# Gate rows spread by DMA instead of TensorE, GLA levels on half the columns, and loads other than weights issued by GpSimd, in an mLSTM + GLA decoder step

## The chip, the cores and the metric

One NeuronCore of one Trainium2 chip runs the whole step. The metric is device time in microseconds of one execution; the numbers given are medians over runs on the chip. All arithmetic is in float32, of which the large matrix products are made from pairs of "fp32r" parts (a rounded high part and the rest).

## The reference, cut to what matters

One layer on 256 prompt tokens and 8 decode sequences of one token each (264 columns in all), model width 2048:

- `p = x @ w_in` with some 13,000 output columns. They feed an mLSTM branch (q, k, v, input and forget gates, output gates), a GLA branch (q, k, v, a low-rank gate, an output gate) and two merge gates.
- mLSTM, 4 heads of 256: `b = cumsum(logf)`, `m_t = max(b + m, max_s(b_t - b_s + itil_s))`, weights `w = exp(b_t - b_s + itil_s - m_t)`, `num = (q k^T * w) v`, `h = num / max(|den|, exp(-m_t))`. With u = b - m (one value per head and prompt token) and r = itil - b, the weight is `exp(u_t + r_s)`: u has to stand in every partition, as a row over t, and so has exp(-m).
- GLA, 4 heads of 128: `a = sum_d q_t k_s exp(bc_t - bc_s)` for s <= t, built here in levels: at level l, blocks of 2^l tokens, each even block s meets the odd block t beside it.
- The decode states (mLSTM C, 8.4 MB; GLA S, 4.2 MB) are read, updated with the new token and written back.
- Norms, gates, two branch projections, the merge, one output projection and a LayerNorm over `ALPHA * x + y`.

## The kernel before, in words

The tokens are columns: x stands in SBUF as 16 tiles of 128 channels by 264 tokens. Output columns of the weights are taken in units of 128; `units()` lists 129 of them (16 qk, 1 small with the gates, 8 av, 4 bq, 4 bk, 8 bv, 16 ao/az, 8 bz, 32 ga/gb, 16 pab, 16 out). A unit is 16 k-tiles of three matmuls each (`parts`, lines 223, 224 and 227: high times high, high times low of x, low times high), that is 48 matmuls of 264 columns.

The weights come as pieces of half a unit (512 KB) through SyncE's queue (`load_raw`, line 181), into four buffers; `cast_piece` makes the high part on ScalarE (line 203) and the rest on VectorE (line 204), into five buffers each, three pieces ahead of the unit that TensorE works on (`LA`).

TensorE's order is the order of the program (`manual_schedule`). The other engines are ordered by a scheduler with priorities, each engine's stream being fixed when the kernel is built. Between two units `pump` moves the side work on: it steps generators, each up to its next `yield`, as far as a budget of 2.8 goes. The generators that matter here:

- `g_gates` (from line 279): gates of the mLSTM. It makes m, b, u, r in 16 partitions (lines 316 to 336), transposes r, and then makes `dmx` = exp(-m) in all 128 partitions by eight matmuls with a selecting matrix `selr` (lines 377 and 378, in two steps with a `yield` after each).
- `g_a_prompt`: mLSTM on the prompt. For each head, `s1` makes the scores (line 420) and beside them spreads u over the partitions by four matmuls with `selr` (line 423); line 427 adds r and the causal limit.
- `g_a_decode`: the decode states, 16 chunks of 512 KB: `load` (line 526), rows of k and q spread from DRAM (`spread_rows`, line 489), decay on ScalarE (line 555), update and product on VectorE (lines 571 and 573), store through GpSimd's queue (line 564).
- `g_gla_prompt`: seven levels; each has its products on TensorE (line 707), scalings of Q and K on VectorE (line 714) and a copy under a mask into `am` (line 730).
- `g_gla_decode`: 8 chunks (`load`, line 778) with rows of three kinds (`rows_of`, line 489), VectorE lines 807 to 810, store through GpSimd (line 813).

All large tiles beside the weights share a pool of 20 slots (`b4`); a load into a slot waits until whatever stood there has been used or stored. All loads go through SyncE's queue, in order, so weights and the loads of the side work stand in one line; GpSimd's queue carries most stores and a few small operations.

Of the kernel before, what the change touches and what calls it, by code (L numbers as in the profile page):

```python
# [13 lines left out]
F32 = mybir.dt.float32  # L14
# [7 lines left out]
L = 256  # L22
# [3 lines left out]
H = 4  # L26
# [57 lines left out]
def body(ctx, tc, xT, wbig, wsmall, par, cmask, lmask, sel, rowc, gate, wgu, cT, sT, nst, cst, lnr,  # L84
# [152 lines left out]
    st, sel_t = {}, {}  # L237
# [41 lines left out]

    def g_gates(ps):  # L280
# [36 lines left out]
        gr = lambda n: tmp.tile([16, T], F32R, tag="t1", name=n, bufs=T1_BUFS)  # L317
        mh_, ml_, uh, ul = gr("mhi"), gr("mlo"), gr("uhi"), gr("ulo")
        selr = t4([16, 8, 128], "selr", F32R)
        A.copy(out=selr, in_=sel_t["sel"])  # L320
# [13 lines left out]
        split(mh_, ml_, m)  # L334
        split(uh[:, 0:L], ul[:, 0:L], u[:, 0:L])
        st.update(uh=uh, ul=ul, selr=selr)
# [4 lines left out]
        for w, src in ((0, r), (1, wk)):  # L341
            for s in range(2):
                o = w * 32 + s * 16
                PE.transpose(out=pt[:, o:o + 16], in_=src[:, s * 128:(s + 1) * 128], identity=ident[0:16, 0:16])
        dm = one.tile([16, H, NB], F32, tag="dm", name="dm")
# [26 lines left out]
        em = t4([128, H, T], "dmx")  # L372
        st["dmx"] = em
        for hh in (0, 2):
            for h in (hh, hh + 1):
                pp = side_ps()[:, 0:T]
                PE.matmul(pp, lhsT=selr[:, h, :], rhs=mh_, start=True, stop=False)
                PE.matmul(pp, lhsT=selr[:, h, :], rhs=ml_, start=False, stop=True)
                A.activation(out=em[:, h, :], in_=pp, func=AF.Exp, scale=-1.0)
            yield 1.0  # L380
# [27 lines left out]
    def g_a_prompt():  # L408
        qT, kT, vt = st["qT"], st["kT"], st["avt"]
        uh, ul, selr, rw, dmx = st["uh"], st["ul"], st["selr"], st["rw"], st["dmx"]  # L410
# [75 lines left out]
    def spread_rows(dst, src):  # L486

        n = src.shape[0] * src.shape[1]
        nc.sync.dma_start(out=dst.rearrange("p b d -> p (b d)"),  # L489
                          in_=src.rearrange("r d -> (r d)").unsqueeze(0).to_broadcast([128, n]))  # L490

    def g_a_decode():
# [14 lines left out]
        nc.sync.dma_start(out=nr, in_=nst)  # L507
# [3 lines left out]
        for x, src in enumerate((kr, qr)):  # L511
            nc.sync.dma_start(out=kq_d[x], in_=src)
# [149 lines left out]
    def g_gla_rows():  # L662
        gq, gk, la = st["gq"], st["gk"], st["la"]
        gd = one.tile([128, 3, H, NB], F32, tag="gd", name="gd")
        A.activation(out=gd[:, 0], in_=la[:, :, L:T], func=AF.Exp, scale=TAU_INV)
        V.tensor_copy(out=gd[:, 1], in_=gk[:, :, L:T])
        V.tensor_copy(out=gd[:, 2], in_=gq[:, :, L:T])
        yield 0.4
        pt = side_ps()
        PE.transpose(out=pt[0:96, 0:128], in_=gd.rearrange("p x h b -> p (x h b)"), identity=ident)  # L670
        rows = tmp.tile([96, 128], F32, tag="t1", name="rows", bufs=T1_BUFS)
        A.copy(out=rows, in_=pt[0:96, 0:128])
        rows_d = dram.tile([96, 128], F32, name="rows_d")
        nc.sync.dma_start(out=rows_d, in_=rows)
        st["rows"] = rows_d
        yield 0.3

    def g_gla_prompt():
# [19 lines left out]
        for l in range(7):  # L698
            hs = 1 << l
            pl = side3(8, 64)  # L700
            for hf in range(2):
                for h in range(H):
                    for s0, n0, w in {32: ((0, 0, 32), (64, 32, 32)), 64: ((0, 0, 64),)}.get(hs, ((0, 0, 64), (64, 0, 64))):
                        m = min(hs, 64) if hs >= 32 else 64
                        rhs = Q[:, h, hf * 128:hf * 128 + 128].rearrange("p (n two s) -> p n two s", two=2, s=hs)[
                            :, n0 // hs:(n0 + w) // hs, 1, :]
                        PE.matmul(pl[s0:s0 + m, 4 * hf + h, n0:n0 + w].rearrange("p (n s) -> p n s", s=hs),  # L707
                                  lhsT=K[:, h, hf * 128 + s0:hf * 128 + s0 + m], rhs=rhs, start=True, stop=True)
# [11 lines left out]
            av = am.rearrange("p a (n two s) -> p a n two s", two=2, s=hs)[:, :, :, 1, :]  # L720
# [5 lines left out]
            if hs == 64:  # L726
# [3 lines left out]
            V.copy_predicated(out=av, mask=lm_sb[:, l, :].rearrange("p (n s) -> p n s", s=hs).unsqueeze(1).to_broadcast(  # L730
                [128, 8, 64 // hs, hs]), data=pl.rearrange("p a (n s) -> p a n s", s=hs))
# [39 lines left out]
    def g_gla_decode():  # L771
# [168 lines left out]
    def g_ln_rows():  # L940
# [3 lines left out]
        for hf in range(2):  # L944
            gf, hi = t4([128, 1024], "lgf"), t4([128, 1024], "lgh", F32R)
            gg = t4([128, 1024], "lgg", F32R)
            nc.sync.dma_start(out=gf, in_=lnr[:, hf * 1024:hf * 1024 + 1024])
# [4 lines left out]
            nc.sync.dma_start(out=bb, in_=lnr[64:65, hf * 1024:hf * 1024 + 1024].to_broadcast([128, 1024]))  # L952
# [150 lines left out]
    with tc.manual_schedule(engines=MANUAL):  # L1103
# [20 lines left out]
        for n, (kind, j) in enumerate(UN):  # L1124
# [15 lines left out]
            else:  # L1140
# [3 lines left out]
                if n == 4:  # L1144
                    V.tensor_copy(out=im_sb, in_=ident)
                    sel_t["sel"] = t4([16, 8, 128], "sel_sb")
                    for dst, src in ((gate_sb, gate), (wgu_sb, wgu), (sel_t["sel"], sel), (rc_sb, rowc), (cm_sb, cmask), (lm_sb, lmask)):
                        nc.sync.dma_start(out=dst, in_=src)
# [41 lines left out]
def _layout(v):  # L1190
# [51 lines left out]
    sel = np.zeros((16, 8, 128), np.float32)  # L1242
    for st in range(2):
        for h in range(4):
            for p in range(128):
                sel[(2 * st + p // 64) * 4 + h, st * 4 + h, p] = 1.0
    d["sel"] = sel
# [63 lines left out]
```

## Time and profile before

| | us |
|---|---|
| median of three runs | 845.92 (845.65 to 849.77) |
| the profiled execution | 848.47 |
| its span, first to last instruction | 846.7 |
| TensorE busy in it | 826.7 (98%) |
| VectorE busy | 591.4 (70%) |
| ScalarE busy | 451.4 (53%) |
| GpSimd busy | 45.1 (5%) |
| share of the span in which the 16 DMA engines moved data of SyncE's queue | 61.3% |
| the same for GpSimd's queue | 4.3% |

The profiled execution lies 1.77 us outside its span (848.47 - 846.7), and 2.55 us above the median. A matmul's record is longer than the distance to the next one, since they are pipelined: it is the starts that tell what one costs.

### The profile page before, as it was taken

How to read it: one execution, taken by the hardware profiler on the slowest of the kernel's cores; microseconds unless marked ns; L12 is line 12 of the kernel's file. 1: busy time of each engine (PE TensorE's matmuls, PEld its weight loads, DVE VectorE, ACT ScalarE, POOL GpSimd, SP SyncE). 2: the span in 40 equal slices, each digit the busy share in tenths (PEclk: the TensorE clock that was granted, in tenths of full speed). 3: DMA queues.
4: the chain of work that ended last, by engine and by line, in shares of the span. 5: the costliest groups of instructions: out<-in, count | busy, mean ns of one | idle time of the engine just before them, and what ended most of it. 6: DMA issues, size and time to landing. Idle time of an engine off the chain costs nothing.

```text
span 846.7 us, 16717 instructions
## 1 busy us (share of the span) xinstructions
PE 826.7 (98%) x6773; PEld 813.3 (96%) x6773; DVE 591.4 (70%) x964; ACT 451.4 (53%) x706; POOL 45.1 (5%) x75
## 2 busy tenths in 40 slices
PE   6999999999999999999999998999999999999996
PEld 6999999999899999999999998999999999999995
DVE  6877668545658788757579979994445766666962
ACT  5655457545445653555467747764444444444633
POOL 0000000000001000001000000310000000000410
PEclk9999999999999999999999998999999999999998
DMA  8765565558586985678687799756555555576513
GB/s 318 246 203 181 159 188 171 165 163 262 214 284 225 381 292 189 198 262 312 203 300 243 231 335 329 240 171 203 184 178 184 185 177 177 185 248 214 176 49 103
DMA packets 54766, 184.76 MB, mean 218 GB/s; under 512 B 8209, under 2 KB 9153, under 8 KB 54689
## 3 DMA queue, kind: packets, MB, share of 16 engines
q1 hardware_dynamic: 50560, 169.28, 61.3%
q0 software_dynamic: 4128, 14.42, 4.3%
q8 instruction: 53, 0.87, 0.4%
q14 instruction: 25, 0.20, 0.1%
HBM read 166.98 MB, written 16.69 MB: 217 GB/s over the span
## 4 chain that ended last, share of the span: by engine, by line
PE 81%; DMA 7%; DVE 6%; ACT 2%; issue 2%; SPq 1%; ACTq 0%; POOLq 0%; POOL 0%; DVEq 0%
PE mm L223 25%; PE mm L224 25%; PE mm L227 24%; DMA raw<-wbig 4%; DMA cch<-cT 4%; DVE lo L204 2%; ACT hi L203 1%; DVE scr L573 1%; PE sd L707 1%; PE sd L464 1%; DVE cch L571 1%; ACT cch L555 1%; PE sd L754 0%; SPq L489 0%; PE sd L420 0%
## 5 line engine op out<-in xcount | busy, mean ns | idle before, releaser
L223 PE MATMUL mm<-xh,hi 128*128 128x264 f32 x1552 | 447.2, 289 | 10.2 <-ACT hi L203 9.8
L224 PE MATMUL mm<-xl,hi 128*128 128x264 f32 x1552 | 441.2, 285 | 0.0
L227 PE MATMUL mm<-xh,lo 128*128 128x264 f32 x1536 | 437.2, 285 | 0.5 <-DVE lo L204 0.5
L203 ACT CAST hi<-raw 128x1024 fp32r<-128x1024 f32 (+1 forms) x260 | 267.9, 1034 | 279.5 <-PE mm L224 245.1
L204 DVE TENSOR_TENSOR lo<-raw,hi 128x1024 fp32r<-128x1024 f32 (+1 forms) x260 | 314.9, 1214 | 144.2 <-ACT hi L203 142.0
L223 PEld LDWEIGHTS mm<-xh,hi 128*128 128x128 f32 x1552 | 294.0, 189 | 12.5 <-ACT hi L203 10.0
L224 PEld LDWEIGHTS mm<-xl,hi 128*128 128x128 f32 x1552 | 294.2, 190 | 0.3
L227 PEld LDWEIGHTS mm<-xh,lo 128*128 128x128 f32 x1536 | 290.1, 189 | 1.0 <-DVE lo L204 1.0
L223 PE MATMUL mm<-mh,hi 128*128 128x264 f32 x256 | 72.9, 285 | 0.0
L224 PE MATMUL mm<-ml,hi 128*128 128x264 f32 x256 | 72.7, 284 | 0.0
L227 PE MATMUL mm<-mh,lo 128*128 128x264 f32 x256 | 72.4, 283 | 0.0
L555 ACT ACTIVATE cch<-cch,decb 128x256 f32<-128x256 f32 x64 | 28.0, 500 | 38.6 <-DMA cch<-cT 38.6
L571 DVE SCALAR_TENSOR_TENSOR cch<-kb,avd,cch 128x256 f32<-128x256 f32 x64 | 29.0, 479 | 27.8 <-ACT cch L555 27.8
L227 PEld LDWEIGHTS mm<-mh,lo 128*128 128x128 f32 x256 | 48.2, 188 | 0.0
L223 PEld LDWEIGHTS mm<-mh,hi 128*128 128x128 f32 x256 | 48.1, 188 | 0.0
L224 PEld LDWEIGHTS mm<-ml,hi 128*128 128x128 f32 x256 | 48.1, 188 | 0.0
L224 PE MATMUL mm<-ybl,hi 128*128 128x264 f32 x128 | 36.4, 284 | 0.0
L227 PE MATMUL mm<-yah,lo 128*128 128x264 f32 x128 | 36.4, 284 | 0.0
L223 PE MATMUL mm<-ybh,hi 128*128 128x264 f32 x128 | 36.4, 284 | 0.0
L224 PE MATMUL mm<-yal,hi 128*128 128x264 f32 x128 | 36.2, 283 | 0.0
L227 PE MATMUL mm<-ybh,lo 128*128 128x264 f32 x128 | 36.2, 283 | 0.0
L223 PE MATMUL mm<-yah,hi 128*128 128x264 f32 x128 | 36.2, 282 | 0.0
(323 smaller groups left out, 820.1 us busy)
## 6 DMA issues: line engine op xcount, KB each, us to landing
raw<-wbig SPq DMA_DIRECT2D x252, 512.0 KB, 4.7
cch<-cT SPq DMA_DIRECT2D x16, 512.0 KB, 8.6
sC<-cch POOLq DMA_DIRECT2D x16, 512.0 KB, 5.8
kb<-kq_d SPq DMA_DIRECT2D x8, 512.0 KB, 7.2
qb<-kq_d SPq DMA_DIRECT2D x8, 512.0 KB, 8.8
sch<-sT SPq DMA_DIRECT2D x8, 512.0 KB, 7.6
sS<-sch POOLq DMA_DIRECT2D x8, 512.0 KB, 6.7
xr<-xT SPq DMA_DIRECT2D x4, 528.0 KB, 7.1
```

The source lines that it names most:

```text
L203: A.copy(out=h, in_=r)
L204: V.tensor_tensor(out=lo, in0=r, in1=f(h), op=ALU.subtract)
L223: PE.matmul(out, lhsT=wh, rhs=rh, start=(k == k0), stop=False)
L224: PE.matmul(out, lhsT=wh, rhs=rl, start=False, stop=small and k == k1 - 1)
L227: PE.matmul(out, lhsT=los[n, k], rhs=rh, start=False, stop=(k == k1 - 1))
L464: PE.matmul(CN[:, 0:VC], lhsT=kw[:, s, d * 128:d * 128 + 128], rhs=vt[h // 2][:, s, h % 2, :], start=(s == 0), stop=(s == 1))
L555: A.activation(out=c[:, b, :], in_=c[:, b, :], func=AF.Copy, scale=decb[:, h, b0 + b:b0 + b + 1])
L571: V.scalar_tensor_tensor(out=c[:, b, :], in0=kb[:, b, :], scalar=avd[:, 2 * h + e, b0 + b:b0 + b + 1], in1=c[:, b, :], op0=ALU.mult, op1=A ...
L573: V.scalar_tensor_tensor(out=scr2, in0=c[:, b, :], scalar=1.0, in1=qb[:, b, :], op0=ALU.mult, op1=ALU.mult, accum_out=nd[:, L + b0 + b:L + ...
L707: PE.matmul(pl[s0:s0 + m, 4 * hf + h, n0:n0 + w].rearrange("p (n s) -> p n s", s=hs), lhsT=K[:, h, hf * 128 + s0:hf * 128 + s0 + m], rhs=r ...
```

## The change

Three edits.

1. Rows u and m of the gates. m (4 x 264) and u (16 x 256) are written to two DRAM tiles and read back with the same row in every partition: `em` (128 partitions x 4 x 264) and two tiles `ub` (128 x 4 x 256, each as two halves of 64 partitions). exp(-m) is then one operation on all of `em`, in one step instead of two. The matmuls with the selecting matrix go (lines 377, 378 and 423), with the matrix, its load, its cast and the splits of m and u.
2. GLA levels of block 1 to 16: each product takes the 32 odd-block columns that belong to the same 64 tokens as its 64 rows, instead of the 64 odd-block columns of 128 tokens; the masked copy is made in two halves of 64 partitions.
3. Loads other than weights go through GpSimd's queue: `spread_rows`, the chunks of both decode parts, `nst`, the rows of the final LayerNorm, and the small stores `kq_d` and `rows_d`. The loads at the start (x, parameters, constants) stay on SyncE's.

```diff
+    def spread_rows(dst, src):
+        n = src.shape[0] * src.shape[1]
+        G.dma_start(out=dst.rearrange("p b d -> p (b d)"),
+                    in_=src.rearrange("r d -> (r d)").unsqueeze(0).to_broadcast([dst.shape[0], n]))
...
-        mh_, ml_, uh, ul = gr("mhi"), gr("mlo"), gr("uhi"), gr("ulo")
-        selr = t4([16, 8, 128], "selr", F32R)
-        A.copy(out=selr, in_=sel_t["sel"])
...
-        split(mh_, ml_, m)
-        split(uh[:, 0:L], ul[:, 0:L], u[:, 0:L])
-        st.update(uh=uh, ul=ul, selr=selr)
+        m_d, u_d = dram.tile([H, T], F32, name="m_d"), dram.tile([16, L], F32, name="u_d")
+        G.dma_start(out=m_d, in_=m[0:H])
+        G.dma_start(out=u_d, in_=u[:, 0:L])
         G.dma_start(out=pm, in_=m[0:H, L - 1:L])
         G.dma_start(out=sm, in_=m[0:H, L:T])
         yield 3.0
...
+        em, ub = t4([128, H, T], "dmx"), [t4([128, H, L], "ub") for _ in range(2)]
+        spread_rows(em, m_d)
+        for s in range(2):
+            for q in range(2):
+                spread_rows(ub[s][q * 64:q * 64 + 64], u_d[(2 * s + q) * H:(2 * s + q) * H + H])
+        st.update(dmx=em, ub=ub)
...
         yield 1.5
-        em = t4([128, H, T], "dmx")
-        st["dmx"] = em
-        for hh in (0, 2):
-            for h in (hh, hh + 1):
-                pp = side_ps()[:, 0:T]
-                PE.matmul(pp, lhsT=selr[:, h, :], rhs=mh_, start=True, stop=False)
-                PE.matmul(pp, lhsT=selr[:, h, :], rhs=ml_, start=False, stop=True)
-                A.activation(out=em[:, h, :], in_=pp, func=AF.Exp, scale=-1.0)
-            yield 1.0
+        A.activation(out=em, in_=em, func=AF.Exp, scale=-1.0)
+        yield 1.0
...
         def s1(h):
-            S, U = side_ps(), side_ps()
-            Us = U[:, 0:L], U[:, L:2 * L]
+            S = side_ps()
             for t0, n, o, s0 in ((0, 256, 0, 0), (128, 128, 256, 128)):
                 for d in range(2):
                     PE.matmul(S[:, o:o + n], lhsT=kT.t(2 * h + d)[:, s0:s0 + 128], rhs=qT.t(2 * h + d)[:, t0:t0 + n],
                               start=(d == 0), stop=(d == 1))
-                for ur in (uh, ul):
-                    PE.matmul(Us[s0 // 128][:, 0:L], lhsT=selr[:, (s0 // 128) * 4 + h, :], rhs=ur[:, 0:L],
-                              start=(ur is uh), stop=(ur is ul))
...
-                V.scalar_tensor_tensor(out=E[:, o:o + n], in0=Us[s][:, L - n:L], scalar=rw[:, 0, s, h:h + 1],
+                V.scalar_tensor_tensor(out=E[:, o:o + n], in0=ub[s][:, h, L - n:L], scalar=rw[:, 0, s, h:h + 1],
...
-                nc.sync.dma_start(out=c, in_=cT[i])
+                G.dma_start(out=c, in_=cT[i])
...
-                    for s0, n0, w in {32: ((0, 0, 32), (64, 32, 32)), 64: ((0, 0, 64),)}.get(hs, ((0, 0, 64), (64, 0, 64))):
+                    for s0, n0, w in ((0, 0, 64),) if hs == 64 else ((0, 0, 32), (64, 32, 32)):
...
-            V.copy_predicated(out=av, mask=lm_sb[:, l, :].rearrange("p (n s) -> p n s", s=hs).unsqueeze(1).to_broadcast(
-                [128, 8, 64 // hs, hs]), data=pl.rearrange("p a (n s) -> p a n s", s=hs))
+            for s0, n0 in ((0, 0), (64, 32)):
+                r = slice(s0, s0 + 64)
+                V.copy_predicated(
+                    out=am[r, :, s0:s0 + 64].rearrange("p a (n two s) -> p a n two s", two=2, s=hs)[:, :, :, 1, :],
+                    mask=lm_sb[r, l, n0:n0 + 32].rearrange("p (n s) -> p n s", s=hs).unsqueeze(1).to_broadcast(
+                        [64, 8, 32 // hs, hs]),
+                    data=pl[r, :, n0:n0 + 32].rearrange("p a (n s) -> p a n s", s=hs))
...
-                nc.sync.dma_start(out=c, in_=sT[i])
+                G.dma_start(out=c, in_=sT[i])
```

## Rows read from the trace of the kernel before

**Rows 1.** The page's busy time, share of the span and instructions of each engine
```profile
PE 826.7 (98%) x6773; PEld 813.3 (96%) x6773; DVE 591.4 (70%) x964; ACT 451.4 (53%) x706; POOL 45.1 (5%) x75
```

**Rows 2.** TensorE's waits: in total, times, longest (us)
```profile
PE mm L223 <- ACT hi L203: 9.8, 2, 7.2
PE sd L707 <- DVE gq L714: 1.5, 1, 1.5
```

**Rows 3.** Stretches: busy us (instructions) by engine, TensorE's granted clock, DMA share, GB/s
```profile
140.00:185.00 45.00, 45.00 (x363) 43.76 (x361) 23.71 (x47) 20.42 (x32) 1.03 (x2) 1.00 0.52 166
...
486.00:500.00 14.00, 14.00 (x119) 14.00 (x118) 11.89 (x17) 7.14 (x17) 0.53 (x1) 1.00 0.89 344
500.00:510.00 10.00, 7.41 (x62) 7.20 (x60) 5.62 (x11) 3.89 (x10) 0.53 (x1) 0.99 0.99 337
...
600.00:700.00 100.00, 100.00 (x827) 100.00 (x827) 57.30 (x72) 44.09 (x54) 0.00 (x0) 1.00 0.57 182
```

**Rows 4.** Chain of waits, side matmuls: start us, duration us, what
```profile
185.25 0.42 PE sd L423 x2
185.68 0.64 PE sd L420 x4
...
324.87 1.08 PE sd L707 x32
...
346.13 0.63 PE sd L707 x32
...
359.85 0.89 PE sd L735 x8
```

**Rows 5.** Timeline of TensorE at the second step of exp(-m)
```profile
171.84 0.38 PE L377 MATMUL sd<-mhi,selr 16*128 16x264 f32 x1
...
172.52 0.39 PE L223 MATMUL mm<-xh,hi 128*128 128x264 f32 x1
```

**Rows 6.** Timeline of TensorE around its longest wait after the start
```profile
507.12 0.28 PE L227 MATMUL mm<-xh,lo 128*128 128x264 f32 x1
510.01 0.59 PE L223 MATMUL mm<-xh,hi 128*128 128x264 f32 x1 [2.60 <-ACT hi L203]
...
516.70 0.29 PE L227 MATMUL mm<-xh,lo 128*128 128x264 f32 x1
```

**Rows 7.** Chain of waits, its transfers ahead of TensorE's two waits
```profile
300.18 9.85 DMA cch<-cT
...
485.76 11.28 DMA raw<-wbig
...
499.90 8.98 DMA raw<-wbig
```

**Rows 8.** Timeline of SyncE's queue, 483 to 503 us
```profile
483.85 2.23 SPq L181 DMA_DIRECT2D raw<-wbig  x2
490.76 0.33 SPq L489 DMA_DIRECT2D ga<-rows_d  x1
497.53 0.33 SPq L489 DMA_DIRECT2D gk<-rows_d  x1
...
499.90 3.25 SPq L181 DMA_DIRECT2D raw<-wbig  x4
```

**Rows 9.** The page's DMA issues: queue, count, KB each, median us to landing
```profile
raw<-wbig SPq DMA_DIRECT2D x252, 512.0 KB, 4.7
cch<-cT SPq DMA_DIRECT2D x16, 512.0 KB, 8.6
sC<-cch POOLq DMA_DIRECT2D x16, 512.0 KB, 5.8
```

**Rows 10.** The masked copies of the levels: duration ns min/median/max
```profile
L730 DVE COPY_PREDICATED am<-lm_sb,sd x5: 711/723/1325, 317.5 to 342.4; 128x512 f32<-128x512 int32 x5
```

**Rows 11.** Waits of ScalarE and VectorE for decode chunks: total, times, longest (us)
```profile
ACT cch L555 <- DMA cch<-cT: 38.6, 13, 6.7
...
DVE sch L807 <- DMA sch<-sT: 3.8, 2, 3.6
```

More of the change, by code (lines that the diff above doesn't have):

```diff
@@ L83, in body @@
 @with_exitstack
-def body(ctx, tc, xT, wbig, wsmall, par, cmask, lmask, sel, rowc, gate, wgu, cT, sT, nst, cst, lnr,
+def body(ctx, tc, xT, wbig, wsmall, par, cmask, lmask, rowc, gate, wgu, cT, sT, nst, cst, lnr,
          y, yd, pC, pn, pm, pconv, pS, sC, sn, sm, sS):
@@ L235, in x_rhs @@
         return x_hi[k // 4][:, k % 4, :], x_lo[k // 4][:, k % 4, :]
-    st, sel_t = {}, {}
+    st = {}
     def g_conv_prep():
@@ L316, in g_gates @@
         m, b, u, r, lm = gt("m"), gt("b"), gt("u"), gt("r"), gt("lm")
-        gr = lambda n: tmp.tile([16, T], F32R, tag="t1", name=n, bufs=T1_BUFS)
-        mh_, ml_, uh, ul = gr("mhi"), gr("mlo"), gr("uhi"), gr("ulo")
-        selr = t4([16, 8, 128], "selr", F32R)
-        A.copy(out=selr, in_=sel_t["sel"])
         V.tensor_tensor(out=u[:, 0:L], in0=logf[:, 0:L], in1=cmk, op=ALU.mult)
@@ L409, in g_a_prompt @@
         qT, kT, vt = st["qT"], st["kT"], st["avt"]
-        uh, ul, selr, rw, dmx = st["uh"], st["ul"], st["selr"], st["rw"], st["dmx"]
+        ub, rw, dmx = st["ub"], st["rw"], st["dmx"]
         num = st["num"]
@@ L484, in g_a_prompt @@
         st["ap_done"] = True
[L486 to L490, printed above, removed]
     def g_a_decode():
@@ L506, in g_a_decode @@
             PE.transpose(out=pt[0:64, x * 128:x * 128 + 128], in_=qkd[:, x].rearrange("p h b t -> p (h b t)"), identity=ident)
-        nc.sync.dma_start(out=nr, in_=nst)
+        G.dma_start(out=nr, in_=nst)
         A.copy(out=qr, in_=pt[0:64, 0:128])
@@ L511, in g_a_decode @@
         for x, src in enumerate((kr, qr)):
-            nc.sync.dma_start(out=kq_d[x], in_=src)
+            G.dma_start(out=kq_d[x], in_=src)
         yield 0.5
@@ L673, in g_gla_rows @@
         rows_d = dram.tile([96, 128], F32, name="rows_d")
-        nc.sync.dma_start(out=rows_d, in_=rows)
+        G.dma_start(out=rows_d, in_=rows)
         st["rows"] = rows_d
@@ L719, in g_gla_prompt @@
             B, nb = B2, n2
-            av = am.rearrange("p a (n two s) -> p a n two s", two=2, s=hs)[:, :, :, 1, :]
             if hs == 32:
@@ L946, in g_ln_rows @@
             gg = t4([128, 1024], "lgg", F32R)
-            nc.sync.dma_start(out=gf, in_=lnr[:, hf * 1024:hf * 1024 + 1024])
+            G.dma_start(out=gf, in_=lnr[:, hf * 1024:hf * 1024 + 1024])
             A.copy(out=hi, in_=gf)
@@ L951, in g_ln_rows @@
             bb = t4([128, 1024], "lbb")
-            nc.sync.dma_start(out=bb, in_=lnr[64:65, hf * 1024:hf * 1024 + 1024].to_broadcast([128, 1024]))
+            G.dma_start(out=bb, in_=lnr[64:65, hf * 1024:hf * 1024 + 1024].to_broadcast([128, 1024]))
             ln["B"].append(bb)
@@ L1145, in body @@
                     V.tensor_copy(out=im_sb, in_=ident)
-                    sel_t["sel"] = t4([16, 8, 128], "sel_sb")
-                    for dst, src in ((gate_sb, gate), (wgu_sb, wgu), (sel_t["sel"], sel), (rc_sb, rowc), (cm_sb, cmask), (lm_sb, lmask)):
+                    for dst, src in ((gate_sb, gate), (wgu_sb, wgu), (rc_sb, rowc), (cm_sb, cmask), (lm_sb, lmask)):
                         nc.sync.dma_start(out=dst, in_=src)
@@ L1241, in _layout @@
     d["lmask"] = lm
[L1242 to L1247, printed above, removed]
     rc = np.zeros((64, 108), np.float32)
@@ L1301 @@
     args = []
-    for name in ("xT", "wbig", "wsmall", "par", "cmask", "lmask", "sel", "rowc", "gate", "wgu", "cT", "sT", "nst", "cst", "lnr"):
+    for name in ("xT", "wbig", "wsmall", "par", "cmask", "lmask", "rowc", "gate", "wgu", "cT", "sT", "nst", "cst", "lnr"):
         a = arrays[name]
```

## The prediction

> **What bounds the kernel now.** I read the page's busy times first: TensorE is busy 98% of the span [rows 1]. The reader is to see that nothing can be gained but by taking work from TensorE or by ending one of its few waits. Next its waits: 9.8 us in two waits for the cast of a weight piece (the longest, 7.2 us, is the start; the other is 2.60 us at 510 us [rows 6]) and 1.5 us at 318 us, where the products of a GLA level wait for VectorE's scaling of Q [rows 2]. Then the stretches: from 600 to 700 us, with no side work to speak of, 827 matmuls in 100 us, so one costs 0.121 us and a piece of 24 of them 2.9 us [rows 3]. Last the timelines around the waits.
>
> The wait at 510 us is dearer than 2.60 us. From 507.12 to 516.70, 9.58 us, 27 matmuls start [rows 6]; at 0.121 us they would take 3.3. So it cost 6.3 us: after the wait TensorE ran at the lower of its two clock levels (1.2 GHz) until about 516.5, with 0.22 us from start to start. Where it comes from: SyncE's queue issued weight pieces until 486.1, then stood before the spread loads ga (490.76) and gk (497.53), whose slots were not free, and issued the next weight piece at 499.90: 13.8 us without one, where one is wanted every 2.9 [rows 8]. The pieces on either side of the gap took 11.28 and 8.98 us to land [rows 7] against a median of 4.7 [rows 9].
>
> **The change part by part.** Sums are made in the profiled execution, 848.47 us.
>
> *u rows.* Eight pairs of spreading matmuls (two a head) go, 0.42 us each by their row: 3.4 us. The score matmuls of 128 columns that stand between two pairs take 0.64 us for four [rows 4], where eight alike elsewhere (128 columns, the level over whole blocks) take 0.89, so 0.45 for four: changing between the two kinds costs about 0.2 us a head, 0.8 for four. I take 4.2 us, bounds 3.4 and 4.2. All of it lies on TensorE's path, for its order is that of the program.
>
> *exp(-m).* The second step runs from 171.84 to 172.52, 0.68 us [rows 5]; there are two: 1.4 us.
>
> *Levels.* Five levels of the form x32 at 1.08 us [rows 4]. The row for what they become is not there: 32 columns against weights 64 wide. The nearest is the level of block 32, also 32 instructions, 32 columns, but weights 32 wide: 0.63 us. If the columns set the time, 5 x 0.45 = 2.2 us go; if the weights do, nothing. I take 2.2, since that row shares the moving side and the count, and keep 0 for the range. The Trainium skill, "TensorE: Matmul & The Clock Gate", section "Back-to-back issue gap", puts a floor of about 25 ns under each small matmul; 32 of them would be 0.80 us and the saving 1.4. The row contradicts it (0.63 us for 32 is 20 ns each), so the row is used. The masked copies on VectorE, 0.72 us each [rows 10], become ten of half the columns and half the partitions: between nothing and 5 x 0.72 = 3.6 us more in VectorE's 30% of idle time, hidden while the pieces cast ahead last (below).
>
> TensorE's work falls by 4.2 + 1.4 + 2.2 = 7.8 us, bounds 4.8 and 7.8.
>
> *What the rows of u and m cost now.* 128 x 1056 and 128 x 1024 x 2 values of four bytes, 1.6 MB, in the stretch from 140 to 185 us, where the DMA engines are at 0.52 and move 166 GB/s [rows 3]: full, by that, they would move 319, so 153 are spare and 1.6 MB takes some 10 us. m and u are ready at about 150, and the first score needs u when `g_a_prompt` starts, at 185 [rows 4]. It starts one unit earlier now (exp(-m) is one step, not two): at about 178. That leaves 28 us for the write, the wait for it and 10 us of loads, with a landing time of 5 to 9 us each [rows 9]. I cost it at nothing; if that cover were gone, the exponential on ScalarE would stand in front of the casts and TensorE would wait by as much as the loads are late. The casts of the selecting matrix and the splits leave ScalarE and VectorE, a gain of no weight.
>
> *Loads through GpSimd.* This takes ga, gk, gq and the chunks out of the line in which the weights stand. SyncE then waits for nothing but its own four buffers, so the gap of 13.8 us cannot arise there: I take all 6.3 us as gone; the other end is 0, if not the order but the DMA engines are short. That is not idle talk: they are at 0.89 and 0.99, 344 and 337 GB/s, in that very stretch [rows 3]. What speaks for the gain is that the backlog stood ahead of the weights in one queue (11.28 us for a piece [rows 7]); in a queue of their own they share with it. The Trainium skill, "DMA: Bandwidth & Descriptors", section "Queues, rings and completion order", says that a DMA engine takes turns between the queues that have work, packet by packet. By that rule the weights get at least half of 340 GB/s, 170, against the 181 that they use (524,288 bytes in 2.9 us): a few per cent short while the burst lasts, which three pieces of lead outlast. No run here shows it yet.
>
> *What queues behind what on GpSimd.* Its order now has loads behind stores that wait for VectorE. A store of chunk i-1 is issued when VectorE has just finished it, and the load behind it is for chunk i+2 or so; two chunks of time stand against a landing of 8.6 us [rows 9]. In the trace of before the chunk loads are already issued after those stores, held up on SyncE. So I cost it at nothing.
>
> *The wait at 318 us.* Its chain holds a chunk load of 9.85 us [rows 7], which may come earlier or later now: 0 to 1.5 us. I leave it where it is in the forecast.
>
> Sum: 848.47 - 7.8 - 6.3 = **834.4 us**. Without the wait at 318 too it is 832.9. The profiled execution lies 2.55 us above the median of 845.92. TensorE's work is the same in each execution, so what differs is waits; a kernel without them should come to 834 in its ordinary runs as well. Should the ordinary runs of before wait less at 510 us, the gain against the median is smaller than the sum, 11.5 and not 14.1, but the end is the same.
>
> **The rivals.**
>
> *B: the wait at 510 us stays, for the DMA engines are full.* For: the 0.99 above. Against: the gap in SyncE's issues comes before it. Time: 848.47 - 7.8 = 840.7.
>
> *C: the levels do not get shorter.* For: the weights stay 64 wide. Against: the row of 0.63. Time: 834.4 + 2.2 = 836.6.
>
> *D: slower; the slot waits move to GpSimd's queue and starve VectorE.* Place: the three changes of head in `g_gla_decode`. The loads ga, gk and gq of the next head wait for slots that a store must free; behind them on GpSimd now stand the stores and the next chunk, so VectorE waits for sch, as it already does for 3.6 us [rows 11], with the casts of the weights behind it in its stream. It decides as soon as such a wait passes the three pieces cast ahead, 8.7 us; ScalarE's longest wait for a chunk so far is 6.7 us [rows 11], within it. Each time costs what the one at 510 us does, 6.3: three of them in place of one, 848.47 - 7.8 + 12.6 = 853.3. The Trainium skill, "SBUF — State Buffer", section "Who interferes with whom", adds that GpSimd cannot write descriptors while VectorE runs a fast copy, which speaks against moving loads there. The stores through GpSimd land in 5.8 us [rows 9] beside a busy VectorE, so the trace does not bear out a large delay.
>
> *E: one new wait as dear as the old arises elsewhere (a chunk late for ScalarE, or the rows of the final norm), and the old one stays.* 840.7 + 6.3 = 847.0.
>
> **How the numbers follow.** Forecast 0.48, B 0.20, C 0.12, D 0.12, E 0.08. Half a per cent, 4.2 us, is about what a measurement of this kernel can tell from no change: faster means below 841.7, slower above 850.1. Forecast and C are faster; B lies near the line and I split it 0.14 to 0.06; E is the same; D is slower, a fifth of it only just not. Faster 0.74, same 0.16, slower 0.10. The range of 8 in 10 goes from 831 (all waits gone, and a little of the start) to 846, so it holds the forecast, C, B and part of E, and leaves out D.
>
> **What would show it.** Right: TensorE's instructions down by 8 for exp(-m) and 16 for u; the five levels near 0.65 us; no gap of more than some 4 us in SyncE's issues between 420 and 545 us; granted clock 1.00 in every stretch until the end; TensorE's idle time down from 20 us to about 17. Wrong: a wait of TensorE for the cast of a piece anywhere after 40 us (B or E, by whether SyncE's queue or the landing of a piece is late), levels still at 1.08 (C), or VectorE waiting for sch or cch for over 8 us (D). The prediction fails if the sum on TensorE is right and the end is still above 841: then the waits were not SyncE's order.

## The result, and the profile after

The changed kernel takes 855.60 us (median of four runs, 853.59 to 858.43) where the kernel before took 846.02 on the same chip: ratio 1.0106, interval 1.0062 to 1.0149 (a ratio here is formed over all runs, so it is near the ratio of the two medians but not equal to it). It is slower by 9.6 us. The forecast was 834.4 and its range ended at 846. The profiled execution after is one of 854.24 us, with a span of 852.4. It lies 1.36 us below its median and the one before 2.45 us above that of 846.02, so the two traces differ by 5.8 us; of the other 3.8 us no trace shows where they are.

The page's busy times come first, as in [rows 1]:

```profile
PE 821.4 (96%) x6749; PEld 811.1 (95%) x6749; DVE 593.7 (70%) x967; ACT 451.2 (53%) x700; POOL 76.7 (9%) x142
```

TensorE has 24 instructions less, the 16 and 8 that were counted, and its busy time is 5.3 us less. The span grew by 5.7 us all the same. So TensorE's idle time rose from 20 to 31 us. Its waits (in total, times, longest; the counterpart of [rows 2]) say where a part of that is:

```profile
PE mm L223 <- ACT hi L203: 6.9, 1, 6.9
PE sd L698 <- DVE gq L705: 6.7, 1, 6.7
PE sd L824 <- DVE ns L819: 2.7, 1, 2.7
```

The first is the start. The wait at 510 us is gone: the stretch there (columns as in [rows 3]) has TensorE full and at the higher clock level.

```profile
140.00:185.00 45.00, 45.00 (x368) 44.41 (x367) 25.18 (x52) 20.94 (x32) 7.34 (x14) 1.00 0.74 215
...
500.00:510.00 10.00, 10.00 (x85) 10.00 (x84) 7.28 (x10) 7.48 (x16) 1.05 (x2) 1.00 0.76 268
```

In its place stand a wait of 6.7 us for the scaling of Q (1.5 before [rows 2]) and one of 2.7 us for a statistic of the second norm (that of the GLA; the first is the mLSTM's). Here is the first in TensorE's timeline:

```profile
317.87 1.92 PE L698 MATMUL sd<-gq,gk 128*64 128x32 f32 x32 [6.74 <-DVE gq L705]
...
320.33 0.42 PE L227 MATMUL mm<-xh,lo 128*128 128x264 f32 x1
...
324.80 0.28 PE L223 MATMUL mm<-xh,hi 128*128 128x264 f32 x1
```

There are two prices: 6.74 us of standing still, and then matmuls of 0.42 us, 0.22 from start to start, at the lower clock level until about 324.4, where the higher one gives 0.12.

What each place costs shows when the start of the same weight matmul is compared in the two timelines (the matmuls of lines 223, 224 and 227, counted from 0; us):

```
matmul   place                    before    after   after less before
 2160    ahead of level 1         312.19   306.51   -5.7
 2304    behind it                335.01   337.95   +2.9
 3456    ahead of 510 us          491.77   494.70   +2.9
 3744    behind it                532.90   529.50   -3.4
 3888    behind the second norm   552.08   553.17   +1.1
 6048    near the end             814.22   815.43   +1.2
```

Ahead of level 1 the change has gained 5.7 us, what the first edit takes from TensorE. The wait there takes 8.6 back. The wait at 510 us does bring its 6.3, as forecast, and the second norm, where the kernel before does not wait, takes 4.5 of them back.

The rest is not on TensorE. SyncE's last store, yd, is issued at 843.27 (842.03 before), 1.2 us later like TensorE's last matmuls. But the span ends 9.1 us behind that store, not 4.7. What runs there is the closing DRAIN on GpSimd's queue (count, then ns min/median/max, first and last start). Before:

```profile
L1307 POOLq DRAIN  x3: 40/93/3394, 841.6 to 846.4; - x3
```

After:

```profile
L1295 POOLq DRAIN  x3: 40/93/8861, 842.8 to 852.2; - x3
```

The chain of waits shows the parts of the change themselves, as in [rows 4]:

```profile
176.60 1.31 PE sd L420 x8
177.91 0.44 PE sd L448 x4
...
327.86 1.05 PE sd L698 x32
```

The scores of a head are eight products in one run of 1.31 us, with no change of kind between them. The levels take 1.05 us, not 0.63.

### The profile page after: what moved, and what is told of

The parts are those of the page before. It is cut to its first block, busy times and chain, and to the rows that moved or that the text cites. A ratio compares the mean times of both kernels' runs of the same rounds, so it can differ in the third digit from the quotient of the medians.

```text
span 852.4 us, 16687 instructions
## 1 busy us (share of the span) xinstructions
PE 821.4 (96%) x6749; PEld 811.1 (95%) x6749; DVE 593.7 (70%) x967; ACT 451.2 (53%) x700; POOL 76.7 (9%) x142
## 4 chain that ended last, share of the span: by engine, by line
PE 80%; DMA 9%; DVE 6%; issue 2%; ACT 1%; POOL 1%; ACTq 0%; POOLq 0%; SPq 0%; DVEq 0%
PE mm L223 25%; PE mm L224 24%; PE mm L227 24%; DMA cch<-cT 4%; DVE lo L204 3%; DMA sch<-sT 2%; DMA raw<-wbig 1%; DMA xr<-xT 1%; PE sd L698 1%; DMA sS<-sch 1%; PE sd L420 1%; PE sd L461 1%; ACT hi L203 1%; DVE gpr L804 1%; DVE scr L564 1%
## 6 DMA issues: line engine op xcount, KB each, us to landing
qb<-kq_d POOLq DMA_DIRECT2D x8, 512.0 KB, 10.6
```

## The experiments

Three theories of the 9.6 us were open after these views. First, the loads through GpSimd cost by themselves, at the end (the drain) and on the way (loads behind waiting stores). Second, what the first edit takes from TensorE is lost at fixed meeting points with VectorE. Third, the levels' copies in halves burden VectorE. The times below are medians, each with its ratio to the kernel before on the same chip and the ratio's interval. A profile is one execution, so its waits differ from those of the others. "First edit" is rows u and m, "second" the levels, "third" the loads through GpSimd.

**e1_rows_only.** The first edit alone.

```diff
+        m_d, u_d = dram.tile([H, T], F32, name="m_d"), dram.tile([16, L], F32, name="u_d")
+        G.dma_start(out=m_d, in_=m[0:H])
+        G.dma_start(out=u_d, in_=u[:, 0:L])
...
-                    PE.matmul(Us[s0 // 128][:, 0:L], lhsT=selr[:, (s0 // 128) * 4 + h, :], rhs=ur[:, 0:L],
-                              start=(ur is uh), stop=(ur is ul))
...
+        spread_rows(em, m_d)
```

> The kernel before with the first edit alone: rows u and m by DMA through GpSimd (7 transfers more there, 42 in all), every other load back on SyncE's queue, levels as before. Theory A (the loads that moved to GpSimd's queue make the wait at level 1 of the GLA and the longer end; the rows themselves are a plain gain): TensorE's side work down by 5.6 us, wait for VectorE's scaling of Q at level 1 at most 2 us, GpSimd's last drain 4.0 us; about 841 to 843 us. Rival B (the gain on TensorE cannot be kept: it comes to level 1 earlier and VectorE's chain ends when it did): that wait grows from 1.5 to about 7 us and the low clock follows; 846 to 850 us.

846.17 against 847.14; 0.9985 [0.9967, 1.0003]: no gain. Of TensorE's waits in it the two largest after the start:

```profile
PE sd L698 <- DVE gq L705: 5.0, 1, 5.0
PE sd L820 <- DVE ns L815: 2.7, 1, 2.7
```

The wait at 510 us is gone without the third edit, and new ones stand at the level (316.8 us; 317.7 before, so the level starts when it always did) and at the norm. TensorE arrives earlier and VectorE doesn't. So rival B of the expectation held, with a wait of 5.0 us where about 7 were expected. This profile is of the longest of the ten executions (849.65); e3 below, with the same first edit, was profiled in an execution of 846.15, and there the two waits are 2.0 and 1.9 us. A third meeting point lies ahead of them, where products wait for ScalarE's `vT`: 1.9 us here, 2.7 in e3, none in the kernel before. By the starts of the weight matmuls e3 is 7.2 us ahead of the kernel before at matmul 1728, 2.3 at 2016 and 0.4 at 2304, behind level 1: the saving is made, and it is gone before 340 us.

**e2_loads_only.** The third edit alone.

```diff
-                nc.sync.dma_start(out=c, in_=sT[i])
+                G.dma_start(out=c, in_=sT[i])
```

> The kernel before with the third edit alone: the loads other than weights through GpSimd's queue (60 transfers more, 95 in all), matmuls with the selecting matrix and levels as before. Theory A: the wait at level 1 is 5 us or more, the wait near 510 us is gone, GpSimd's last drain is 8.3 us; 855 to 860 us, since TensorE's side work is not reduced. Rival B (what moved level 1 is the earlier arrival of TensorE and of the decode, by the first edit): wait at level 1 as before, 1.5 us, wait near 510 us gone; 843 to 846 us with the longer drain.

856.39 against 847.14; 1.0117 [1.0086, 1.0148]: all of the loss, from this edit alone. Theory A had the time, but not by its reasons: the wait at level 1 is 0.8 us, not 5, and the one near 510 us is there. SyncE's queue now holds weights only, and TensorE waits near 510 us all the same, for longer than before and with the lower clock level behind it (0.83 granted on average from 500 to 520 us):

```profile
512.34 0.59 PE L227 MATMUL mm<-xh,lo 128*128 128x264 f32 x1 [3.15 <-DVE lo L204]
```

The chain of waits ahead of it (start, us, what):

```profile
482.22 0.52 POOL gq L489
482.74 13.03 DMA sch<-sT
...
500.09 1.15 DVE lo L204
...
501.25 8.74 DMA raw<-wbig
...
510.07 1.05 ACT hi L203
```

To be read downwards: GpSimd issues a chunk behind the rows gq, it takes 13 us to land, VectorE waits for it with the casts behind it in its stream; the cast at 500.09 frees a weight buffer, only then can SyncE issue the next piece (501.25), and this lands late too. The DMA engines are full there (last two columns: share, GB/s):

```profile
490.00:500.00 10.00, 10.00 (x85) 10.00 (x85) 5.81 (x8) 6.00 (x11) 1.08 (x3) 1.00 1.01 392
```

GpSimd's queue now has the waits for slots (waited for, in total, times, longest), and VectorE's wait for the chunks grows from 3.8 us [rows 11] to 11.4:

```profile
POOL sch L778 <- DMA sS<-sch: 9.0, 1, 9.0
POOL ga L489 <- DVE gpr L809: 7.1, 1, 7.1
```

```profile
DVE sch L807 <- DMA sch<-sT: 11.4, 3, 4.5
```

That is rival D's place and its mechanism, with rival B's full engines at its end. But it is not what makes this kernel slower, for the kernel before pays the same at 510 us: e2 is 1.4 us ahead of it at matmul 3456 and still 1.1 at 3744. Then comes the second norm, TensorE's largest wait here after the start:

```profile
PE sd L829 <- DVE ns L824: 4.2, 1, 4.2
```

At matmul 3888 e2 is 4.8 us behind, so the norm costs 5.9. The chain there leads back through VectorE's work on the chunks to a load that GpSimd issued at 516.77 and that took 8.46 us to land. The other 3.9 us stand at the end, where the span ends 8.6 us behind the last store and not 4.7.

**e3_rows_levels.** First and second edit, loads on SyncE as before (the diff is the third edit undone).

```diff
-                G.dma_start(out=c, in_=cT[i])
+                nc.sync.dma_start(out=c, in_=cT[i])
```

> The changed kernel with its loads (all but the rows of u and m) back on SyncE's queue: first and second edit. If the second edit gives nothing on TensorE, as 1.05 us a level against 1.08 says, and its ten masked copies cost VectorE little: within 1 us of the run with the first edit alone. If the ten copies delay the levels: 1 to 4 us slower than that.

846.29 against 847.14; 0.9992 [0.9976, 1.0008]. It equals e1, so the second edit is worth nothing that can be measured, and its copies in halves cost nothing that can be.

**e4_tiny_dmas.** The kernel before, with 66 tiny writes to DRAM on GpSimd's queue that nothing waits for.

```diff
+            if kind in ("ga", "gb") and 4 <= j < 15:
+                for z in range(3):
+                    G.dma_start(out=tiny_d[tn[0]], in_=ones[0:16, 0:8])
+                    tn[0] += 1
```

> The kernel before, with 66 writes of 16 x 8 values to a scratch tensor in DRAM through GpSimd's queue, three a unit between 550 and 700 us, where that queue is idle: 101 transfers in all there, as many as in the changed kernel, but hardly any bytes. If the drain of GpSimd at the end costs by the number of transfers (0.08 us each: 3.39 us with 35, 8.86 with 102): 8.8 us of drain and about 5.4 us more in all, 851 us. If it costs by packets or bytes (4128 packets and 14.4 MB against 12848 and 45.5 MB): drain 3.4 to 4.0 us and 846 us.

850.20 against 847.14; 1.0043 [1.0031, 1.0054]. The drain is 8.78 us with writes of 32 bytes from each of 16 partitions, so it goes by the number of transfers and not by their bytes. The time rose by 3.1 us, not by the 5.4 expected; 4.4 of the drain show behind the last store, which the interval allows. One kernel for each count, with the two runs e12 and e13 that were foretold from this line (GpSimd's transfers counted from the code; last store and end of span from the trace; us):

```
kernel   transfers   drain   last store   end of span   between
before       35      3.394     842.03        846.7        4.7
e9           42      3.964     835.15        839.9        4.8
e13          72      6.414     838.73        845.4        6.7
e12          78      6.901     847.88        855.2        7.3
e2           95      8.289     846.67        855.3        8.6
e4          101      8.781     838.71        847.8        9.1
after       102      8.861     843.27        852.4        9.1
```

The drain is 0.54 + 0.0816 us for each transfer; the other eight traces have 35, 42 or 102 transfers and the drain of their count within 0.01 us. Up to about 42 it hides behind the landing of the last store, 4.7 us; at 102 it shows with 4.4 us.

**e5_rows_later, e6_all_later, e7_before_later.** To see whether the first edit's gain is lost at the meeting points, level 1 starts two units later and the norm's first statistic three: e5 has the first edit, e6 the whole change, e7 none of it.

```diff
+            if l == 1:
+                for _ in range(2):
+                    yield 0.0
...
+        for _ in range(3):
+            yield 0.0
         for h in range(H):
             vp = side_ps()[:, 0:T]
```

> The run with the first edit alone, and TensorE's two meeting points with VectorE put later in its order: level 1 of the GLA two units later, the first statistic of the GLA norm three units later. Theory B (the 5.6 us taken from TensorE came back as waits at those two points, 5.0 and 2.7 us, and as low clock after them): both waits under 1 us, granted clock 1.00 from 40 us on; 834 to 838 us. Rival (VectorE is short of time as such between 440 and 545 us): the wait shows up elsewhere, for a cast of a weight piece; 842 us or more.

> The changed kernel, all three edits, with the same two points later. Theory: its waits of 6.7 and 2.75 us go, and what is left against the run with the rows alone and later points is the drain of GpSimd, 8.9 us against 4.0, of which some 4 show: 838 to 843 us. If loads through GpSimd cost more than the drain (late chunks that hold ScalarE or VectorE and so the casts): 845 us or more.

> The kernel before with only the two points later, no edit of the change. Theory B: its 1.5 us at level 1 go, the wait near 510 us is for a cast and may stay: 841 to 846 us, and at least 4 us slower than the run with the rows of u and m as well. If the later points do it all and the rows give nothing: equal to that run.

Against 845.55: e5 843.82, 0.9978 [0.9964, 0.9991]; e6 850.37, 1.0049 [1.0029, 1.0070]; e7 846.24, 0.9994 [0.9971, 1.0018]. So e5 and e6 missed their theories (834 to 838 and 838 to 843; for e6 the other branch, 845 or more, came), and e5 is 2.4 us below e7, not 4. The norm's wait went in e5; the level's moved on to level 2. TensorE in e5:

```profile
335.99 1.98 PE L701 MATMUL sd<-gq,gk 128*64 128x64 f32 x32 [5.79 <-DVE gq L708]
```

What held VectorE, from ScalarE's timeline of e5 and then VectorE's:

```profile
327.98 1.71 ACT L546 ACTIVATE cch<-cch,decb 128x256 f32<-128x256 f32 x4 [8.62 <-DMA cch<-cT]
```

```profile
328.52 0.88 DVE L562 SCALAR_TENSOR_TENSOR cch<-kb,avd,cch 128x256 f32<-128x256 f32 x2 [6.51 <-ACT cch L546]
...
335.16 0.69 DVE L708 TENSOR_TENSOR gq<-gq,gE 128x512 f32<-128x512 f32 x1
```

Both engines work in order. A chunk pair of `g_a_decode` that lands late stops ScalarE for 8.6 us; VectorE's work on it, and behind that the scaling which TensorE needs, come 6.5 us late. Two units more only let the next pair come in between. The kernel without any edit has the same wait in this order, 5.2 us at 339.50 in e7, so it is not the first edit that makes it. The next step was therefore to take the chunks out from among the levels.

**e8_forms.** The first edit with 192 more small products, 32 of each of six forms, in the unit steps behind the levels; their results are not used.

```diff
+        for wr, wc in ((64, 64), (64, 32), (64, 16), (32, 64), (32, 32), (32, 16)):
+            ...
+                PE.matmul(fm[s0:s0 + wr, i // 2, 0:wc], lhsT=K[...64 * (i % 2) + wr], rhs=Q[...128 + wc], start=True, stop=True)
```

> The run with the first edit alone, and after the levels six bursts of 16 more products (32 instructions) each, whose results nobody uses: weights 64 wide with 64, 32 and 16 columns, then weights 32 wide with 64, 32 and 16. If the weights set the time: 1.05 to 1.08 us for the first three, 0.63 for the last three. If the columns do: 1.08, 0.63 and less by columns, whatever the width. If neither below some floor: 64 wide 1.08, 1.05, 1.05 and 32 wide near 1.05, 0.63, 0.63.

The chain of waits has one row for each form (start, us), in the order of the diff:

```profile
365.04 1.08 PE sd L729 x32
377.91 1.06 PE sd L729 x32
390.77 1.04 PE sd L729 x32
403.62 1.02 PE sd L729 x32
417.33 0.63 PE sd L729 x32
432.43 0.62 PE sd L729 x32
```

Halving the columns alone takes 2%, halving the weights alone 6%, both together 42%. The second edit halves the columns only. (The kernel with them took 850.42 in its one run.)

**e9_rows_paused, e10_all_paused, e11_before_paused.** No chunks among the levels: `g_a_decode` is held back from the start of `g_gla_prompt` to the end of its levels, and the norm's statistic is three units later. e9 has the first edit, e10 the whole change, e11 none of it.

```diff
+        st["levels"] = True
         am = t4([128, 8, 128], "am")
...
+        del st["levels"]
         pl = side3(4, 128)
...
-            for g in [g for g in side if g.__name__ in BACK][:1]:
+            for g in [g for g in side if g.__name__ in BACK and "levels" not in st][:1]:
```

> The kernel before with rows u and m loaded (the first edit alone), and two changes of order: the work of g_a_decode is held back from the start of g_gla_prompt until its seven levels are done, and b_norm's first statistic product stands three units later. Theory (the 5.6 us that the first edit takes from TensorE come back as waits because the scaling of a level stands in VectorE's queue behind the chunks of g_a_decode): the waits at the levels (5.0 us at 316.8 in the first edit alone, 5.8 us at 336 where level 1 was moved) and the one at the norm (2.7 us) all go, TensorE waits for under 4 us in all after its start, and the time is 836 to 840, ratio to before 0.988 to 0.994. Rival (TensorE meets VectorE and the casts again elsewhere, because both have as much to do and g_a_decode now ends two units later): one or more new waits of 2 to 6 us after 350 us, time 842 to 846, ratio over 0.995.

> The whole change with the same two changes of order. Theory (the third edit costs by itself: about 4 us at the end that show of the 8.8 us drain of GpSimd's queue, and one to two waits for casts): 4 to 6.5 us above the run with the first edit alone in the same order, so 840 to 846, and the drain 8.8 to 8.9 us. Rival (the third edit hurts only through the meeting points at the levels and the norm): within 2 us of that run.

> The kernel before with the same two changes of order and none of the three edits. Theory (with the meeting points moved out of the way the first edit is worth what it takes from TensorE, 5.6 us): 4 to 6 us above the run with rows u and m loaded in this order, so 841 to 845, its ratio to before 0.993 to 0.999. Rival (the order alone does it, the rows are worth nothing): within 1.5 us of that run.

Against 846.45: e9 839.75, 0.9923 [0.9898, 0.9947], faster than both kernels; e10 854.72, 1.0107 [1.0079, 1.0135]; e11 847.68, 1.0012 [0.9993, 1.0030]. TensorE's largest waits in e9, the start's first:

```profile
PE mm L223 <- ACT hi L203: 7.6, 2, 7.4
PE sd L401 <- ACT vT L394: 3.8, 2, 2.9
PE mm L227 <- DVE lo L204: 1.8, 2, 1.0
```

In e11:

```profile
PE mm L223 <- ACT hi L203: 7.4, 1, 7.4
PE sd L648 <- DVE ns L641: 4.5, 2, 3.0
```

In e10:

```profile
PE mm L223 <- ACT hi L203: 7.2, 1, 7.2
PE sd L639 <- DVE ns L632: 3.8, 2, 3.0
PE mm L227 <- DVE lo L204: 3.3, 2, 2.0
PE sd L699 <- DVE gq L706: 3.1, 1, 3.1
```

In e9 the waits at the levels and at both norms are gone, and its time is within the 836 to 840 of its theory, though TensorE waits 6.6 us after its start and not under 4. It is 7.9 us below e11 where 4 to 6 were expected. Whether that is the first edit's saving is not shown. TensorE waits for `vT` in e9, 3.8 us, and with that its lead over e11 shrinks from 5.5 us at matmul 1728 to 1.2 at 2160. It grows to 8.2 at 3168, across the first norm, where e11 stands 4.5 us and e9 doesn't. So e9's lead comes from a wait that e11 has and e9 hasn't, and why e9 hasn't it was not tried. The order alone gains nothing (e11).

The third edit costs 15.0 us here (e10 less e9), where 4 to 6.5 were expected: that expectation failed. The drain shows with 4.4 of it. The last store is issued 8.9 us later. The starts of the matmuls say where: e10 is 3.7 us ahead of e9 at matmul 2160, 0.9 behind at 2304 (the level), as much at 3024, and 7.7 behind at 3168, so 6.8 of it are the first norm.

The wait at the level is not the work of a load that leaves late. The last chunk ahead of the levels leaves GpSimd's queue at 290.92 in e10, behind a store that waited 3.2 us for VectorE, and SyncE's at 293.61 in e9. ScalarE goes on with it at the same time in both, first e10, then e9:

```profile
303.48 1.71 ACT L546 ACTIVATE cch<-cch,decb 128x256 f32<-128x256 f32 x4 [12.12 <-DMA cch<-cT]
303.53 1.71 ACT L546 ACTIVATE cch<-cch,decb 128x256 f32<-128x256 f32 x4 [8.15 <-DMA cch<-cT]
```

Level 1 starts at 313.70 in e10 and at 314.22 in e9. At the first norm it is the weights that come late. The first rows below are GpSimd's in e10, the third is from the chain of waits that ends at the norm, and the last is TensorE's:

```profile
417.40 0.53 POOL L568 DMA_DIRECT2D sC<-cch  x1 [13.52 <-DVE cch L562]
417.92 0.53 POOL L775 DMA_DIRECT2D sch<-sT  x1
...
422.93 14.74 DMA raw<-wbig
...
448.93 1.22 PE L639 MATMUL sd<-ns,inv 128*128 128x264 f32 x2 [2.98 <-DVE ns L632]
```

A store waits 13.5 us for VectorE, and behind it seven loads of 512 KB leave within 4 us (417.92 to 421.57). A weight piece issued at 422.93, with only weights in its queue, then takes 14.74 us to land. GpSimd's queue (q0) and SyncE's (q1) from 420 to 438 us (packets, MB, share of the 16 engines):

```profile
q0 software_dynamic: 1090, 3.98, 61.5%
q1 hardware_dynamic: 695, 2.55, 37.0%
```

**e12_chunks_on_sp, e13_rows_on_sp.** e10 with one half of the third edit undone: the 24 chunk loads back on SyncE (e12), or the 30 transfers of k and q rows (e13).

```diff
-                G.dma_start(out=c, in_=cT[i])
+                nc.sync.dma_start(out=c, in_=cT[i])
...
-                    spread_rows(x, rows[32 * i + 8 * h:32 * i + 8 * h + 8, :])
+                    spread_rows(x, rows[32 * i + 8 * h:32 * i + 8 * h + 8, :], nc.sync)
```

> The whole change in the order that holds g_a_decode back, with the 24 chunk loads of cT and sT alone back on SyncE's queue. GpSimd then issues 78 transfers, so by the line through the drains seen so far its last one takes 6.9 us (0.54 and 78 times 0.0816), 2 less than with all 102. Theory that the chunk loads behind waiting stores cost the rest: TensorE's waits of 3.1 us at the levels and 3.0 us at the first norm go, and the time is 841 to 845. Theory that the rows of k and q cost it: the waits stay and the time is 850 to 853, the drain alone being shorter. If both are needed for a wait to come, either half alone gains most of it.

> The whole change in the same order, with the 30 transfers of k and q rows of both decode parts (two writes to DRAM, 28 spreading loads) alone back on SyncE's queue, and the chunk loads on GpSimd's. GpSimd then issues 72 transfers and its last drain takes 6.4 us, 2.4 less than with all 102. Theory that the chunk loads behind waiting stores cost the rest: TensorE's waits stay, 848 to 853. Theory that the rows of k and q cost it: they go, 840 to 845.

Against 847.44: e12 855.90, 1.0114 [1.0089, 1.0138]; e13 849.44, 1.0033 [1.0016, 1.0049]. Both drains came out as foretold, 6.90 and 6.41 us. The theory that the chunk loads cost the rest fell by e12, whose time no branch had foretold: without them GpSimd's queue is no better a place. That e13 came out at the time which the same theory gave it is then no support for it. Taking the rows of k and q back is worth about 6 us by the ratios (1.0107 in e10), of which 2.5 are the drain's (9.2 less 6.7 behind the last store). But e13 isn't free of waits. The longest is one for a cast:

```profile
519.83 0.59 PE L227 MATMUL mm<-xh,lo 128*128 128x264 f32 x1 [5.82 <-DVE lo L204]
```

SyncE's queue has a gap again ahead of it, as in the kernel before: two weight pieces leave in the 18 us from 482.3 to 500.37, for the rows stand in its line. But ScalarE's casts had caught up by 511 us. What ended last is a chunk on GpSimd's queue: its load waited there 8.15 us for VectorE, and then VectorE stood 7.49 us with the casts behind it in its stream:

```profile
510.36 1.04 POOL L775 DMA_DIRECT2D sch<-sT  x2 [8.15 <-DVE sch L805]
...
517.35 0.69 DVE L804 TENSOR_TENSOR sch<-sch,ga 128x512 f32<-128x512 f32 x1 [7.49 <-issue]
```

The last row names no releaser, but the chunk takes 6.9 us to land and so is there at 517.3. The gap used up pieces cast ahead and the late chunk did the rest; how much either is worth alone was not tried. In e12 all of the loss against e9 lies at the first norm (13.2 us by the starts of the matmuls, 9.4 of waits). There, too, six rows leave GpSimd's queue together, from 419.52 to 422.13, and ScalarE then stands 5.9 us for a weight piece. But e11, with every such load on SyncE, has a wait at this norm as well, so not all of it is the rows'. Neither half by itself is the cause.

## Why the prediction was wrong

**The step that failed** is "Loads through GpSimd": it was put down as a gain of 6.3 us with no cost. The edit alone costs 9.2 us (e2), and three things in that step were wrong.

- *A term was missing.* The closing drain of GpSimd's queue was never reckoned with, though the trace of before has its row, 3.39 us. With 67 more transfers (60 of them from this edit) it is 8.86 us and shows with 4.4. That is settled: it follows the count in all fifteen traces, e12 and e13 were foretold from it, and tiny transfers alone bring it (e4).
- *The weights' share was taken for safe.* "In a queue of their own they share with it" was reckoned as at least 170 GB/s, a few per cent short while a burst lasts. The Trainium skill, "DMA: Bandwidth & Descriptors", section "Queues, rings and completion order", says that a DMA engine takes turns between the queues with work, and that number was worked out from it. Measured from 420 to 438 us in e10, the weights had 37.0% of the engines' time and 142 GB/s (2.55 MB in 18 us), and a piece took 14.74 us; the measurement decides. In the changed kernel itself the weights came in time (its only wait of TensorE for a cast after the start is 0.3 us), so there this did not cost.
- *The 6.3 us were added to the end.* The wait at 510 us went, and TensorE gained 6.3 us there, as forecast. 4.5 of them came back as a wait and low clock at the second norm, where VectorE is later than TensorE once TensorE is not held up at 510. And SyncE's order alone was not the cause: with weights only in its line the wait came all the same (e2), for SyncE waits for buffers that VectorE's casts free, and VectorE waited for a chunk. "SyncE then waits for nothing but its own four buffers" was true, and these were what came late. The wait is not there in e1, where SyncE's line is as before and the decode work begins one unit earlier; why that is enough was not tried by itself.

That stores of GpSimd's queue wait for VectorE was costed at nothing. For the one load that can be compared, the dates bear that out: the chunk ahead of the levels leaves at 290.92 in e10, 293.61 in e9 and 291.22 in e1. ScalarE's longest wait for a chunk did rise from 6.7 us [rows 11] to 12.4, past the 8.7 us of the three pieces cast ahead. It stands ahead of level 1 in the changed kernel, and ScalarE goes on at 303.77, where it does so at 302.35 in e1 and 301.46 in e3. With the visible drain taken off, the edit costs 5.3 us by e2, 2.1 by e6 less e5 and 10.6 by e10 less e9. For the first norm in e10 the chain of waits names a weight piece behind a burst of loads; which load makes the other waits is open.

**The second step that failed** is the sum itself: "All of it lies on TensorE's path". The work went, the end did not move (e1, 0.9985): the saving is there at matmul 1728 and is gone behind level 1, since at `vT`, at level 1 and at the norm TensorE waits for ScalarE or VectorE, whose dates the edit hardly changes. The row stood in [rows 2]: 1.5 us at the level in the kernel before. It meant that VectorE was already the later of the two there, so that what TensorE saves ahead of that point can come back as waiting. The prediction left that wait "where it is" and should have let it grow by the saving; it grew to 6.7. An order in which the saving reaches the end was not shown: e9 is 6.7 us faster than the kernel before, but in its trace it is 3.5 us ahead at matmul 3168 and gains 5.3 more from the wait at 510 us, which it hasn't, as e1 and e11 haven't, before it loses some at later casts.

**Levels.** 2.2 us was the end of the range taken; it is 5 x 0.03 = 0.15. The row of 0.63 us differed in two things, columns and weights, and the choice let one of them stand for both; e8 shows that neither does it alone. Rival C was right on this. The Trainium skill, "TensorE: Matmul & The Clock Gate", section "Back-to-back issue gap", gives small matmuls a floor of some 25 ns; here 32 took 0.62 us at the smallest form, about 20 ns each and so below it, and 33 ns in the form that the edit makes. So the floor was not the right price either.

**What was right.** The rows of u: a head's scores went from 2.35 us to 1.31, 4.2 us for four, as worked out with the change of kind. The 2.35 are the two pieces of [rows 4] and the two beside them:

```profile
184.39 0.86 PE sd L420 x4
...
186.32 0.43 PE sd L423 x2
```

The two steps of exp(-m) are gone. The rows of u and m cost TensorE nothing where they are loaded: it is full from 140 to 185 us, with the DMA engines at 0.74. The forecast's own sign of failure came: the sum on TensorE was right but for the levels, and the end is above 841. Rival D's 853.3 came within 2.3 us of the result by luck. In the changed kernel TensorE has no wait in the decode of the GLA, which was D's place, and VectorE's longest wait for a chunk there is 4.5 us; D had three waits of 6.3 us and no drain, where two waits elsewhere and the drain made up the time. It was given 0.12.

## What to carry to other kernels

Before work or a wait is taken from the busiest engine, look for the next point where it meets another one, however short the wait there: here most of each saving ended at such a point. Comparing the start of the same instruction in two traces shows it, place by place. Loads moved to a second queue still share the engines with the first: here a burst of them held a weight piece for 14.74 us. Count the transfers of GpSimd's queue, for the program's end pays for their number.

## What the runs showed of the hardware that was not expected

- The closing drain of GpSimd's queue: 0.0816 us for each transfer issued there, plus 0.54, from 35 to 102 transfers, whatever their size, and with 66 of them issued before 700 us (e4). The span ends 4.7 us behind the last store with 35 transfers and 9.1 with 102.
- Two queues on full engines: the one with only weights had 37.0% of their time and the other 61.5% (e10, 420 to 438 us), and a piece of 512 KB took 14.74 us to land, against a median of 4.6.
- 32 small products in two groups of rows: 1.08 us with weights and columns 64 wide, 1.04 with columns of 16, 1.02 with weights of 32, and 0.63 with both at 32.
